# Eleven instead of ten Strassen pairs in a 256-token FFN's down projection, two by two, and re-ordered stage ends, on one Trainium2 core

## The chip, the core and the metric

One Trainium2 core runs the whole program in one launch. The metric is device microseconds (us) from launch to end, lower is better. The engines are named as in the profile: PE (TensorE matmul) with PEld (its weight loads), DVE (VectorE), ACT (ScalarE), POOL (GpSimd), and SP, whose queue issues the loads of the weights.

## The reference

One encoder layer on 256 tokens of 2048 features, all in float32. A half-step FFN, a mixer (gated linear recurrence beside windowed attention), and a second half-step FFN; RMS norms stand before and behind each.

```
x: [1, 256, 2048]     D_FF = 5632
swiglu(x, w_gate_up, w_down):
    gate, up = split(x @ w_gate_up, 2)           # 2048 -> 2 x 5632
    return (silu(gate) * up) @ w_down            # 5632 -> 2048
x = x + 0.5 * rms_norm(swiglu(rms_norm(x, g1), ...), p1)
p = rms_norm(x, gm) @ w_mix_in                   # 2048 -> 6656
x = x + rms_norm(concat(hgrn2(p), attention(p)) @ w_mix_out, pm)
x = x + 0.5 * rms_norm(swiglu(rms_norm(x, g2), ...), p2)
```

Here the change touches the product with `w_down` in both FFNs, and the stretches between stages, in which the norm of a finished stage meets the first products of the next.

## The kernel before

**Products.** An fp32 product is made of three matmuls on split operands: every weight tile `raw` is cast to a rounded part `h` by ACT (L176), DVE subtracts to get the rest `l` (L177), and PE multiplies h·h, h·l and l·h (`three`, L423 in the profile). A plain *pair* `u` is 256 rows of weights (two tiles of 128 rows) times 1024 columns: 2 tiles x 2 blocks of 128 tokens x 2 blocks of 512 columns x 3, that is 24 matmuls of 128x512. A pair can instead go as a *seven* (`seven`): a scheme of Strassen's kind on the 2x2x2 blocks takes seven block products instead of eight, so 21 matmuls. For that, DVE forms sums of weight blocks first: one addition of 1024 columns (L455) and two of 512 (L459, L461), each in place in `raw`, and each followed by a further cast and split. Its left operands are sums of the activations: they are formed once (`sums_of`, L380 to L384, three DVE operations) and split into `sp` at each use, unless the pair is in `keep`, in which case the split of run 0 is kept for run 1. Four of the seven products gather in banks of their own, which `fold` (L489 and on, eight DVE additions and an ACT copy) adds into the result behind the last seven of a run.

**Down projection.** `Pairs` walks the 22 pairs of `w_down` twice: run 0 makes columns 0 to 1023, run 1 columns 1024 to 2047. `orders` gives the order of the pairs in each run, by hand. The even pairs below 20 (`MIXED`, ten of them) are sevens; the lists alternate a plain pair and a seven, up to the last few. With `AHEAD`, a seven begins the split of the plain pair behind it, so its DVE work is mixed with that pair's. The last two pairs of run 1 are held back for the end (`HELD`). All loads are issued by SP into a ring of `raw` buffers.

**Stage ends.** `finish` writes out by hand what stands in a row on PE, DVE and ACT. It finishes the four banks of run 1 one by one, squares and sums them (`squares`), multiplies by the gain (`gains`), adds the normed result to the residual X in blocks of 128x512 (`update(m, q)`, L666), turns X by PE transposes (`turned`, L210), and takes from the turned blocks the two split parts of X^T: the upper ones on ACT (`hi`, L227), the lower ones on DVE (`lo`, L232). Between these, `lead` brings the next stage's weights (`lead.more` splits them) and its first products (`lead.pieces`, L352 to L354 in the mixer's). There are two such ends, in which a next stage follows: behind the first FFN (end 1) and behind the mixer (end 2). `pre_stats` squares X (`jk`, L249 on ACT, eight blocks) for the next norm; in the FFNs its result reaches PE by `spread`, a product with a diagonal matrix `dg` (L267, L268).

Of the kernel before, what the change touches and what calls it, by code (L numbers as in the profile page):

```python
# [37 lines left out]
def hymba_layer_kernel(  # L38
# [204 lines left out]

    def pre_stats_now():
        for m in range(2):
            ssq = stat.tile([P, 4], F32, tag="ssq", name=nm("ssq"))
            for q in range(4):
                jk = stat.tile([P, 512], BF16, tag="jk", name=nm("jk"), bufs=1)
                nc.scalar.activation(  # L249
                    jk, res["X"][:, m, q * 512 : (q + 1) * 512], AF.Square, accum_out=ssq[:, q : q + 1]  # L250
                )
            r = rsqrt_of(ssq, 1.0 / D, EPS)
            last["rs2"] = nc.vector.tensor_copy(rs2[:, m : m + 1], r)
# [286 lines left out]
    class Pairs(Blocks):  # L540
# [90 lines left out]
        def finish(self, mul, post, new_x=None, gain=None, lead=None):  # L631
# [88 lines left out]
            def lo(m, q):  # L720
                take_lo(m, q, gain, xt, banks[m, q])

            with tc.manual_schedule(engines=ordered):
                products(0, 0, every)
                squares(0, 0)
                gains(0, 0)
                products(0, 1, every)
                squares(0, 1)
                update(0, 0)
                gains(0, 1)  # L730
                products(1, 0, every)
                lead.more(0)
                update(0, 1)
                squares(1, 0)
                gains(1, 0)
                products(1, 1, slice(0, 3))

                def took(m, q):
                    hi(m, q)
                    lo(m, q)  # L740

                turned(0, 0)
                took(0, 0)
                products(1, 1, slice(3, None))
                turned(0, 1)
                squares(1, 1)
                took(0, 1)
                update(1, 0)
                update(1, 1)
                lead.more(1)  # L750
                first, second = lead.pieces(0, xt), lead.pieces(1, xt)
                next(first)
                next(first)
                turned(1, 0)
                took(1, 0)
                gains(1, 1)
                next(first)
                turned(1, 1)
                took(1, 1)
                for _ in first:  # L760
                    pass
                for m, q in ((0, 2), (1, 2), (0, 3), (1, 3)):
                    update(m, q)
                    next(second)
                    turned(m, q)
                    took(m, q)
                for _ in second:
                    pass
# [19 lines left out]
    MIXED = range(0, 20, 2)  # L788
# [48 lines left out]
    def ffn(gated, w_dn, post_gain, again, gain=None, lead=None, aside=None):  # L837

        with ExitStack() as st:
# [10 lines left out]
            def sums_room(u):  # L850
                n = MIXED.index(u)
                if n == 0:
                    where_X_was.append(xp.tile([P, 8, 4, P], F32, tag="X", name=nm("sums")))
                if n < 8:
                    return where_X_was[0][:, n]
                return work.tile([P, 4, P], F32, tag=f"su{n}", name=nm("su"))
# [57 lines left out]
            for g in range(NG):  # L914
# [18 lines left out]
                [1, 0, 3, 2, 5, 4, 7, 6, 9, 8, 11, 10, 13, 12, 15, 14, 17, 16, 18, 19, 20, 21],  # L933

                [1, 0, 3, 2, 5, 4, 7, 6, 9, 8, 11, 10, 12, 13, 14, 15, 16, 18, 17, 19, 20, 21],
            ]
            rows = Pairs(w_dn, orders, hts, sums, work, post_gain, keep=(10, 12, 16))
# [18 lines left out]
    with tc.manual_schedule():  # L956
# [54 lines left out]
        gated.parts[1] = split(raws[0])  # L1011
        turned(0, 1)
# [6 lines left out]
        gated.parts[2] = split(raws[1])  # L1019
        for k in range(2):  # L1020
# [506 lines left out]
```

## Time and profile before

| | us |
|---|---|
| median of 3 runs | 1853.87 (1853.67 to 1853.91) |
| the profiled execution | 1853.69 |
| its span, first to last instruction | 1851.4 |
| PE busy | 1836.2 |
| DVE busy | 1559.9 |
| ACT busy | 1079.3 |
| DMA moved | 365.78 MB, a mean of 198 GB/s |

The profiled execution is 0.18 us below the median, and 2.29 us of it lie outside the span. The stages can be told by the weights that are loaded and by the lines: FFN 1's gate and up projection to about 488 us, its down projection in two runs to about 599 and 704, end 1 to 745, the mixer to 1123 with end 2 behind it to 1155, FFN 2's gate and up to 1614, its down projection to the end. PE is busy nearly throughout, so the time is read as PE's work plus the gaps in it. A gap is read from the starts: matmuls that follow one another start 0.227 us apart, and what a start is later than that is lost. A bracket behind a row names the idle time ahead of it and what ended it.

### The profile page before, as it was taken

Reading aid. Unit: us, or ns where it says so; the run is one execution under the profiler, and the core shown is the slowest. Engines: PE = TensorE matmul, PEld = TensorE weight load, DVE = VectorE, ACT = ScalarE, POOL = GpSimd, SP = SyncE. Lnnn points to the kernel's source line nnn. Section 1 sums busy time; section 2 is a strip of 40 time slices with the busy share of each in tenths; the row PEclk is TensorE's granted clock in tenths of the full one; section 3 lists DMA queues with packets and bytes.
Section 4 is the critical chain, followed back from the end, with each engine's and each line's share of the span. In section 5 each row is a group of like instructions: output and inputs, shape, how many; then the busy total and the mean of one; then the engine's idle time right before and its main releaser. Section 6 shows DMA issues by size and latency. Waiting matters only on the chain.

```text
span 1851.4 us, 23247 instructions
## 1 busy us (share of the span) xinstructions
PE 1836.2 (99%) x8670; PEld 1533.2 (83%) x8670; DVE 1559.9 (84%) x1956; ACT 1079.3 (58%) x1429; POOL 20.6 (1%) x39
## 2 busy tenths in 40 slices
PE   9999999999999999999999999999999999999998
PEld 7888888888888887888888887888888888888886
DVE  7988888888899998577787788888888788899997
ACT  6555555555565655577677655655555555566563
POOL 1000000000000000000000000000000000000000
PEclk9999999999999999999999999999999999999999
DMA  7555555555565565555565555565555555555564
GB/s 253 205 197 189 205 204 182 182 190 200 190 227 212 198 255 197 194 177 166 169 186 157 172 208 200 182 214 186 210 206 194 204 184 206 190 183 207 217 249 156
DMA packets 180881, 365.78 MB, mean 198 GB/s; under 512 B 9257, under 2 KB 56449, under 8 KB 180001
## 3 DMA queue, kind: packets, MB, share of 16 engines
q1 hardware_dynamic: 180416, 364.17, 56.5%
q8 instruction: 68, 1.11, 0.2%
q14 instruction: 45, 0.36, 0.1%
q0 software_dynamic: 352, 0.14, 0.0%
HBM read 360.06 MB, written 4.21 MB: 197 GB/s over the span
## 4 chain that ended last, share of the span: by engine, by line
PE 95%; DVE 2%; ACT 1%; DMA 1%; issue 1%; POOL 0%; SPq 0%; DVEq 0%; ACTq 0%; POOLq 0%
PE pa L423 40%; PE pb L423 37%; PE pa L299 8%; PE pa L304 4%; PE pa L354 1%; PE pa L352 1%; PE pa L353 1%; DVE l L177 1%; PE pa L896 0%; PE pb L896 0%; ACT xt L227 0%; PE pb L1270 0%; PE pb L1248 0%; PE pb L1396 0%; ACT jk L249 0%
## 5 line engine op out<-in xcount | busy, mean ns | idle before, releaser
L176 ACT CAST h<-raw 128x1024 fp32r<-128x1024 f32 (+1 forms) x789 | 796.3, 1029 | 626.9 <-PE pb L423 344.4
L177 DVE TENSOR_TENSOR l<-raw,h 128x1024 fp32r<-128x1024 f32 (+1 forms) x789 | 923.3, 1193 | 202.7 <-ACT h L176 169.2
L423 PE MATMUL pa<-h,xt 128*128 128x512 f32 x1248 | 431.5, 392 | 0.0
L423 PE MATMUL pb<-h,xt 128*128 128x512 f32 x1168 | 407.2, 390 | 0.0
L423 PEld LDWEIGHTS pa<-h,xt 128*128 128x128 f32 x1248 | 234.4, 188 | 48.8 <-ACT h L176 0.8
L423 PEld LDWEIGHTS pb<-h,xt 128*128 128x128 f32 x1168 | 219.2, 188 | 45.5
L423 PE MATMUL pa<-l,xt 128*128 128x512 f32 x624 | 243.2, 390 | 0.0
L423 PE MATMUL pb<-l,xt 128*128 128x512 f32 x584 | 227.3, 389 | 0.0
L299 PE MATMUL pa<-xt,h 128*128 128x512 f32 x672 | 164.7, 394 | 0.0
L423 PE MATMUL pa<-h,ht 128*128 128x512 f32 x464 | 162.7, 389 | 0.0
L423 PE MATMUL pb<-h,ht 128*128 128x512 f32 x464 | 162.6, 389 | 0.0
L299 PEld LDWEIGHTS pa<-xt,h 128*128 128x128 f32 x672 | 123.0, 188 | 23.6
L423 PEld LDWEIGHTS pa<-l,xt 128*128 128x128 f32 x624 | 117.4, 188 | 23.8 <-DVE l L177 0.5
L423 PEld LDWEIGHTS pb<-l,xt 128*128 128x128 f32 x584 | 109.7, 188 | 22.6
L455 DVE TENSOR_TENSOR raw<-raw 128x1024 f32<-128x1024 f32 x84 | 102.8, 1223 | 2.2
L423 PEld LDWEIGHTS pa<-h,ht 128*128 128x128 f32 x464 | 87.1, 188 | 18.2
L423 PEld LDWEIGHTS pb<-h,ht 128*128 128x128 f32 x464 | 87.1, 188 | 18.0
L304 PE MATMUL pa<-xt,l 128*128 128x256 f32 x672 | 91.5, 285 | 0.0
L423 PE MATMUL pa<-l,ht 128*128 128x512 f32 x232 | 90.3, 389 | 0.0
L423 PE MATMUL pb<-l,ht 128*128 128x512 f32 x232 | 90.3, 389 | 0.0
L304 PEld LDWEIGHTS pa<-xt,l 128*128 128x128 f32 x672 | 87.1, 191 | 3.2
L423 PE MATMUL pb<-h,sp 128*128 128x512 f32 x176 | 61.8, 390 | 0.0
(280 smaller groups left out, 2133.0 us busy)
## 6 DMA issues: line engine op xcount, KB each, us to landing
raw<-in_w_ffn_gate_up_dram SPq DMA_DIRECT2D x350, 512.0 KB, 4.7
raw<-in_w_ffn_down_dram SPq DMA_DIRECT2D x88, 1024.0 KB, 5.0
raw<-in_w_mix_in_dram SPq DMA_DIRECT2D x52, 1024.0 KB, 4.9
raw<-in_w_mix_out_dram SPq DMA_DIRECT2D x16, 1024.0 KB, 5.0
pg<-in_post_norm_ffn_dram SPq DMA_DIRECT2D x4, 512.0 KB, 5.8
X<-in_x_dram SPq DMA_DIRECT2D x2, 1024.0 KB, 7.3
bias<-row SPq DMA_DIRECT2D x16, 128.0 KB, 4.6
kept<-X SPq DMA_DIRECT2D x2, 1024.0 KB, 4.8
```

The lines of the kernel that those rows point to most:

```text
L176: nc.scalar.copy(hi, src)
L177: nc.vector.tensor_tensor(lo, src, hi.bitcast(F32), ALU.subtract)
L299: nc.tensor.matmul(slot[f], weights(hs, kk, f), xcol(xt, k), start=(k == 0), stop=(k == KT - 1))
L304: nc.tensor.matmul(slot[f][:, 0:T], weights(ls, kk, f), xcol(xt, kh * 8 + kk, 0), start=False, stop=False,)
L352: nc.tensor.matmul(dst, xh, h[:, o : o + n], start=(k == 0), stop=False)
L353: nc.tensor.matmul(dst, xh, l[:, o : o + n], start=False, stop=False)
L354: nc.tensor.matmul(dst, xl, h[:, o : o + n], start=False, stop=(k == KT - 1))
L423: nc.tensor.matmul(self.bank(at), lhs, rhs, start=(n == 1), stop=n in (ends, self.of[at]), skip_group_check=n > ends,)
L455: nc.vector.tensor_tensor(four[:, 0:2], four[:, 0::3], four[:, 1:2].to_broadcast([P, 2, 512]), ALU.add)
```

## The change

**Down projection.** `MIXED` has eleven pairs, so pair 20 becomes a seven as well, in both runs of both FFNs. The orders no longer alternate: in run 0 the sevens 2 and 4, 8 and 10, 14 and 16, 18 and 20 stand two in a row, in run 1 2 and 4, 8 and 10, 14 and 16, 18 and 20. `keep` has two pairs instead of three. The sums of pair 20 have a place of their own (`su` in the far pool), reserved by `sums[NU - 2] = None` before `Pairs` asks which pairs are sevens.

**Ends.** The four lower parts of a block can be taken two by two (`js`), and the updates of X are placed between them, ahead of the first products of the next stage that need them; `lead.more` comes earlier.

**Squares.** `square_x(m, q)` squares one block of X at any place; `pre_stats_now` squares only the blocks that are left. Four of eight are squared within the ends, two of eight near the start of the kernel.

```
-    MIXED = range(0, 20, 2)
+    MIXED = range(0, 22, 2)
...
+                if u >= NU - 2:
+                    return far["pool"].tile([P, 4, P], F32, tag="su", name=nm("su"), bufs=1)
...
-                [1, 0, 3, 2, 5, 4, 7, 6, 9, 8, 11, 10, 12, 13, 14, 15, 16, 18, 17, 19, 20, 21],
+                [1, 0, 3, 2, 4, 5, 6, 7, 8, 10, 9, 12, 11, 14, 16, 13, 18, 20, 15, 17, 19, 21],
             ]
-            rows = Pairs(w_dn, orders, hts, sums, work, post_gain, keep=(10, 12, 16))
+
+            sums[NU - 2] = None
+            rows = Pairs(w_dn, orders, hts, sums, work, post_gain, keep=(4, 10))
...
+    squared = {}
+    def square_x(m, q):
+        if m not in squared:
+            squared[m] = (stat.tile([P, 4], F32, tag="ssq", name=nm("ssq")), set())
+        ssq, done = squared[m]
+        if q not in done:
+            done.add(q)
...
     def pre_stats_now():
         for m in range(2):
...
-            r = rsqrt_of(ssq, 1.0 / D, EPS)
+                square_x(m, q)
+            r = rsqrt_of(squared.pop(m)[0], 1.0 / D, EPS)
...
                 products(1, 1, slice(0, 3))
...
+                hi(0, 1)
+                square_x(0, 0)
+                square_x(0, 1)
+                lo(0, 0, (2, 3))
+                lo(0, 1, (0, 1))
+                update(1, 0)
+                lo(0, 1, (2, 3))
+                update(1, 1)
+                update(0, 2)
+                update(0, 3)
...
+                gains(1, 1)
+                lo(1, 1)
+                update(1, 2)
+                update(1, 3)
+                for m, q in ((0, 2), (1, 2), (0, 3), (1, 3)):
+                    next(second)
+                    turned(m, q)
                     hi(m, q)
                     lo(m, q)
...
                 for m, q in ((0, 2), (1, 2), (0, 3), (1, 3)):
-                    update(m, q)
-                    next(second)
-                    turned(m, q)
-                    took(m, q)
...
         gated.parts[1] = split(raws[0])
+        square_x(0, 0)
...
         gated.parts[2] = split(raws[1])
+        square_x(1, 0)
```

**DVE, the last sevens of run 1 in FFN 1, before.** `la` and `l` are rests of weight tiles, `raw<-raw` the additions on weight blocks, here of pairs 16 (`raw_5603`) and 18 (`raw_5645`); the last three rows belong to plain pairs.

```order
L461 TENSOR_TENSOR raw_5603<-raw_5603 128x512
L177 TENSOR_TENSOR la_5648<-raw_5645,ha_5647 128x512
L455 TENSOR_TENSOR raw_5645<-raw_5645 128x1024
L177 TENSOR_TENSOR l_5621<-raw_5603,h_5620 128x1024
L177 TENSOR_TENSOR l_5653<-raw_5645,h_5652 128x1024
L459 TENSOR_TENSOR raw_5645<-raw_5645 128x512
L177 TENSOR_TENSOR l_5658<-raw_5645,h_5657 128x1024
L461 TENSOR_TENSOR raw_5645<-raw_5645 128x512
L177 TENSOR_TENSOR l_5663<-raw_5645,h_5662 128x1024
L177 TENSOR_TENSOR l_5697<-raw_5694,h_5696 128x1024
L177 TENSOR_TENSOR l_5701<-raw_5694,h_5700 128x1024
L177 TENSOR_TENSOR l_5731<-raw_5728,h_5730 128x1024
```

The same place after, with pairs 18 (`raw_5631`) and 20 (`raw_5676`):

```order
L471 TENSOR_TENSOR raw_5631<-raw_5631 128x512
L177 TENSOR_TENSOR la_5679<-raw_5676,ha_5678 128x512
L465 TENSOR_TENSOR raw_5676<-raw_5676 128x1024
L177 TENSOR_TENSOR l_5649<-raw_5631,h_5648 128x1024
L177 TENSOR_TENSOR l_5684<-raw_5676,h_5683 128x1024
L177 TENSOR_TENSOR l_5689<-raw_5676,h_5688 128x1024
L469 TENSOR_TENSOR raw_5676<-raw_5676 128x512
L471 TENSOR_TENSOR raw_5676<-raw_5676 128x512
L177 TENSOR_TENSOR l_5694<-raw_5676,h_5693 128x1024
L177 TENSOR_TENSOR l_5728<-raw_5725,h_5727 128x1024
```

In both, the last split of the last seven (`l_5663`, `l_5694`) stands right behind its last addition, with an ACT cast of the sum between the two. What moved: both middle splits now stand ahead of the two 512-wide additions, where one of them stood between them, and after `l_5694` only plain pairs' splits and `fold` are left.

**DVE, end 1, before.** `X` rows are the updates, `xt` rows the lower parts of X^T, `l` rows the splits of the mixer's weights.

```order
L666 SCALAR_TENSOR_TENSOR X_5795<-y_5738,r_5850,X_5795 128x512
L177 TENSOR_TENSOR l_6126<-raw_6123,h_6125 128x1024
L177 TENSOR_TENSOR l_6130<-raw_6123,h_6129 128x1024
L232 SCALAR_TENSOR_TENSOR xt_5814<-pa_5984,cols,xt_5814 128x128 x4
L666 SCALAR_TENSOR_TENSOR X_5795<-y_5738,r_5910,X_5795 128x512
L177 TENSOR_TENSOR l_6160<-raw_6157,h_6159 128x1024
L232 SCALAR_TENSOR_TENSOR xt_5814<-pb_6004,cols,xt_5814 128x128 x4
L666 SCALAR_TENSOR_TENSOR X_5795<-y_5738,r_5850,X_5795 128x512
L177 TENSOR_TENSOR l_6164<-raw_6157,h_6163 128x1024
```

The same stretch after:

```order
L232 SCALAR_TENSOR_TENSOR xt_5844<-pa_5932,cols,xt_5844 128x128 x2
L676 SCALAR_TENSOR_TENSOR X_5826<-y_4904,r_5943,X_5826 128x512
L232 SCALAR_TENSOR_TENSOR xt_5844<-pa_5932,cols,xt_5844 128x128 x2
L676 SCALAR_TENSOR_TENSOR X_5826<-y_4904,r_5943,X_5826 128x512
L676 SCALAR_TENSOR_TENSOR X_5826<-y_5769,r_5885,X_5826 128x512 x2
L232 SCALAR_TENSOR_TENSOR xt_5844<-pb_5982,cols,xt_5844 128x128 x4
L629 TENSOR_TENSOR y_5769<-pb_4989,pg_5824 128x512
L232 SCALAR_TENSOR_TENSOR xt_5844<-pb_6001,cols,xt_5844 128x128 x4
L676 SCALAR_TENSOR_TENSOR X_5826<-y_5769,r_5943,X_5826 128x512 x2
L177 TENSOR_TENSOR l_6161<-raw_6154,h_6160 128x1024
```

The last four updates have moved from between the weight splits and the second half's lower parts to ahead of them.

**ACT, near the start of the kernel, before and after.** `h` rows are casts of weights, `xt` rows the upper parts of X^T.

```order
L176 CAST h_211<-raw_137 128x1024
L227 ACTIVATE xt_123<-pa_215,gain_102 128x128 x4
L227 ACTIVATE xt_123<-pb_220,gain_102 128x128 x4
L176 CAST h_265<-raw_142 128x1024
L176 CAST h_269<-raw_142 128x1024
L176 CAST h_396<-raw_393 128x1024
```

```order
L176 CAST h_211<-raw_137 128x1024
L254 ACTIVATE jk_216,ssq_215<-X_75 128x512
L227 ACTIVATE xt_123<-pa_218,gain_102 128x128 x4
L227 ACTIVATE xt_123<-pb_223,gain_102 128x128 x4
L176 CAST h_268<-raw_142 128x1024
L176 CAST h_272<-raw_142 128x1024
L254 ACTIVATE jk_277,ssq_276<-X_75 128x512
L176 CAST h_396<-raw_393 128x1024
```

Two squares (`jk`) of eight have moved ahead of casts and upper parts; the other six stand some rows later, where all eight stood.

## Rows read from the trace of the kernel before

**Rows 1.** Windows: span and busy us per engine, run 0 and run 1.

```profile
core 0: us, PE busy (x) PEld busy (x) DVE busy (x) ACT busy (x) POOL busy (x), PEclk, DMA share, GB/s
494.60:594.10 99.50, 99.50 (x441) 82.10 (x440) 96.61 (x107) 60.76 (x68) 0.00 (x0) 1.00 0.58 212
594.20:704.10 109.90, 109.90 (x486) 91.01 (x485) 104.16 (x112) 67.32 (x79) 0.00 (x0) 1.00 0.63 226
```

**Rows 2.** Chain that ended last: start, us, engine, line, a pair's 24 matmuls.

```profile
1831.94 5.44 PE pa L423 x24
```

**Rows 3.** Groups by form, run 1, DVE: count, busy us, mean ns, idle before.

```profile
L177 DVE TENSOR_TENSOR l<-raw,h 128x1024 fp32r<-128x1024 f32 x55 | 66.1, 1219 | 4.3 <-ACT h L176 4.1
L455 DVE TENSOR_TENSOR raw<-raw 128x1024 f32<-128x1024 f32 x10 | 12.2, 1224 | 0.3
L177 DVE TENSOR_TENSOR sp<-sums,sp 128x512 fp32r<-128x512 f32 x5 | 3.4, 684 | 0.0
```

**Rows 4.** Timeline of DVE late in run 1: start, us, operation, [idle <-releaser].

```profile
689.39 4.63 DVE L177 TENSOR_TENSOR l<-raw,h 128x1024 fp32r<-128x1024 f32 x4 [1.20 <-ACT h L176]
698.07 0.69 DVE L500 TENSOR_TENSOR pa<-pa,y 128x512 f32<-128x512 f32 x1
698.67 0.69 DVE L501 TENSOR_TENSOR pb<-pb,y 128x512 f32<-128x512 f32 x1
```

**Rows 5.** One line's instructions, L380: duration min/median/max in ns.

```profile
L380 DVE TENSOR_TENSOR su<-z x4: 416/418/419, 410.8 to 1580.2; 128x256 f32<-128x256 f32 x4
```

**Rows 6.** Timeline: a last split in run 0, its reader; that of run 1.

```profile
574.61 1.23 DVE L177 TENSOR_TENSOR l<-raw,h 128x1024 fp32r<-128x1024 f32 x1
...
580.17 0.39 PE L423 MATMUL pb<-l,sp 128*128 128x512 f32 x1
...
692.37 0.39 PE L423 MATMUL pb<-l,sp 128*128 128x512 f32 x1
```

**Rows 7.** Timeline of PE around the two spreads, FFN 1 and FFN 2.

```profile
39.24 0.39 PE L423 MATMUL pa<-h,xt 128*128 128x512 f32 x1
40.32 0.71 PE L268 MATMUL pb<-dg,ones 128*128 128x128 f32 x4 [0.69 <-DVE dg L267]
...
1167.37 0.39 PE L423 MATMUL pb<-h,xt 128*128 128x512 f32 x1
1168.52 0.71 PE L268 MATMUL pb<-dg,ones 128*128 128x128 f32 x4 [0.76 <-DVE dg L267]
```

**Rows 8.** One line's instructions, the squares of X on ACT, duration in ns.

```profile
L249 ACT ACTIVATE jk<-X x24: 620/632/649, 29.6 to 1166.0; 128x512 bf16<-128x512 f32 x24
```

**Rows 9.** Timeline of ACT near the start of the kernel.

```profile
14.88 1.14 ACT L227 ACTIVATE xt<-pa,gain 128x128 fp32r<-128x128 f32 x4 [0.93 <-PE pa L210]
```

**Rows 10.** Timeline of PE in end 1, two transposes of X.

```profile
718.98 0.39 PE L354 MATMUL pa<-h,xt 128*128 128x512 f32 x1
719.85 0.66 PE L210 MATMUL pb<-ident,X 128*128 128x128 f32 x4 [0.49 <-DVE X L666]
...
731.92 0.39 PE L354 MATMUL pa<-h,xt 128*128 128x512 f32 x1
733.52 0.66 PE L210 MATMUL pa<-ident,X 128*128 128x128 f32 x4 [1.21 <-DVE X L666]
```

**Rows 11.** Timeline of PE in end 2, a transpose of X.

```profile
1137.41 0.39 PE L423 MATMUL pa<-h,xt 128*128 128x512 f32 x1
1138.28 0.66 PE L210 MATMUL pb<-ident,X 128*128 128x128 f32 x4 [0.49 <-DVE X L666]
```

**Rows 12.** Timeline of ACT and PE early in FFN 2's run 0.

```profile
1632.49 2.00 ACT L176 CAST h<-raw 128x1024 fp32r<-128x1024 f32 x2 [4.62 <-DMA raw<-in_w_ffn_down_dram]
...
1634.69 0.61 PE L423 MATMUL pb<-h,sp 128*128 128x512 f32 x2
1635.99 0.50 PE L423 MATMUL pb<-l,sp 128*128 128x512 f32 x1 [0.68 <-DVE l L177]
```

**Rows 13.** Windows: the stretch behind end 1's longest wait, columns as in Rows 1.

```profile
733.50:745.00 11.50, 11.48 (x55) 9.55 (x56) 8.62 (x17) 9.54 (x23) 2.19 (x5) 1.00 0.67 228
```

More of the change, by code (lines that the diff above doesn't have):

```diff
@@ L242, in pre_stats @@
             pre_stats_now()
+    squared = {}
[5 more added lines that the diff above has]
+            done.add(q)
+            jk = stat.tile([P, 512], BF16, tag="jk", name=nm("jk"), bufs=1)
+            nc.scalar.activation(
+                jk, res["X"][:, m, q * 512 : (q + 1) * 512], AF.Square, accum_out=ssq[:, q : q + 1]
+            )
     def pre_stats_now():
         for m in range(2):
-            ssq = stat.tile([P, 4], F32, tag="ssq", name=nm("ssq"))
             for q in range(4):
[L248 to L251, printed above, removed]
-            r = rsqrt_of(ssq, 1.0 / D, EPS)
+                square_x(m, q)
+            r = rsqrt_of(squared.pop(m)[0], 1.0 / D, EPS)
             last["rs2"] = nc.vector.tensor_copy(rs2[:, m : m + 1], r)
@@ L718, in hi, with lo @@
                 take_hi(m, q, gain, xt, banks[m, q])
-            def lo(m, q):
-                take_lo(m, q, gain, xt, banks[m, q])
+            def lo(m, q, js=range(4)):
+                take_lo(m, q, gain, xt, banks[m, q], js)
             with tc.manual_schedule(engines=ordered):
@@ L726, in finish @@
                 gains(0, 0)
+                lead.more(0)
                 products(0, 1, every)
                 squares(0, 1)
+                lead.more(1)
                 update(0, 0)
@@ L731, in finish @@
                 products(1, 0, every)
-                lead.more(0)
                 update(0, 1)
@@ L736, in finish @@
                 products(1, 1, slice(0, 3))
-                def took(m, q):
+                turned(0, 0)
+                hi(0, 0)
+                products(1, 1, slice(3, None))
+                lo(0, 0, (0, 1))
+                turned(0, 1)
+                squares(1, 1)
+                hi(0, 1)
[8 more added lines that the diff above has]
+                update(0, 3)
+                first, second = lead.pieces(0, xt), lead.pieces(1, xt)
+                for _ in range(3):
+                    next(first)
+                turned(1, 0)
+                hi(1, 0)
+                next(first)
+                lo(1, 0)
+                turned(1, 1)
+                hi(1, 1)
+                square_x(1, 0)
+                square_x(1, 1)
+                gains(1, 1)
[5 more added lines that the diff above has]
+                    turned(m, q)
                     hi(m, q)
                     lo(m, q)
[L742 to L762, printed above, removed]
-                    update(m, q)
-                    next(second)
-                    turned(m, q)
-                    took(m, q)
-                for _ in second:
+                for _ in (*first, *second):
                     pass
@@ L932, in ffn @@
             orders = [
-                [1, 0, 3, 2, 5, 4, 7, 6, 9, 8, 11, 10, 13, 12, 15, 14, 17, 16, 18, 19, 20, 21],
-                [1, 0, 3, 2, 5, 4, 7, 6, 9, 8, 11, 10, 12, 13, 14, 15, 16, 18, 17, 19, 20, 21],
-            ]
-            rows = Pairs(w_dn, orders, hts, sums, work, post_gain, keep=(10, 12, 16))
+                [1, 3, 0, 5, 2, 4, 7, 6, 9, 8, 10, 11, 12, 13, 14, 16, 15, 18, 20, 17, 19, 21],
+                [1, 0, 3, 2, 4, 5, 6, 7, 8, 10, 9, 12, 11, 14, 16, 13, 18, 20, 15, 17, 19, 21],
+            ]
+            sums[NU - 2] = None
+            rows = Pairs(w_dn, orders, hts, sums, work, post_gain, keep=(4, 10))
             rows.half_gain(far["pool"])
@@ L1019, in hymba_layer_kernel @@
         gated.parts[2] = split(raws[1])
+        square_x(1, 0)
         for k in range(2):
```

## The prediction

> **What bounds the kernel now.** I first read the windows over the two runs of FFN 1's down projection [rows 1]: PE is busy 99.50 of 99.50 us and 109.90 of 109.90, so the time there is PE's number of matmuls times their pace. The pace comes from the chain that ended last: 24 matmuls of a plain pair in 5.44 us, or 0.227 each [rows 2]. The reader should then look at VectorE in the same windows: 96.61 and 104.16 us. It is the second engine, 2.89 and 5.74 us from being the first. So whatever takes matmuls from PE and gives additions to VectorE is limited by these two differences, and by how early VectorE finishes an operand before PE reads it, its lead. Outside the runs PE has a few gaps: one at each spread of the norm [rows 7], and some at the two ends, where a transpose waits for an update of X [rows 10, 11]. These are what the other two parts of the change can take.
>
> **Part 1: twelve matmuls fewer.** Pair 20 goes as 21 matmuls instead of 24, in two runs of two FFNs: 4 x 3 = 12, at 0.227 that is -2.72 us. All of it lies on PE, which is the path. The loads are the same in size and number; only their order on SP's queue changes.
>
> **Part 1, what VectorE pays.** Operations of 1024 columns follow one another at (4.63 - 1.22) / 3 = 1.137 us, those of 512 at 0.60 [rows 3, 4]. A plain pair needs two splits, 2.27 us. A seven needs the addition L455 and three splits of 1024, and four operations of 512 (`la`, L459, L461, `sp`): 4 x 1.137 + 4 x 0.60 = 6.95 us. The new seven costs VectorE 4.68 us more in each run. Run 0 also gets the activation sums of pair 20, since these are formed when the down projection has begun: three operations of at most 0.42 [rows 5], between 0.6 and 1.25, I take 1.0. In run 1 one pair fewer has its split kept: +0.60. PE meanwhile is 3 x 0.227 = 0.68 shorter. So VectorE falls behind PE by 4.68 + 1.0 + 0.68 = 6.36 us more in run 0, and by 4.68 + 0.60 + 0.68 = 5.96 in run 1.
>
> What is there to meet this? First the lead. In run 0 a seven's last split ends at 574.61 + 1.23 = 575.84 and is read at 580.17: 4.33 us early. In run 1 that of the last seven ends at about 690.61 (the first of the four in a row) and is read at 692.37: 1.76 early [rows 4, 6]. Second the idle time, 2.89 and 5.74. If none of the idle time can be used, 6.36 - 4.33 = 2.03 and 5.96 - 1.76 = 4.20 are left, 6.2 us for one FFN. If all of it can, nothing is left: 2.03 is below 2.89 and 4.20 below 5.74. A gain is excluded here, as PE has no gap in these windows that could close. I take the middle, 3.1 for one FFN: of run 1's idle time 4.1 us stands ahead of splits that wait for ACT's cast [rows 3]. Where VectorE is late these casts are done by the time it comes and the idle time vanishes by itself; but the last wait of 1.20 [rows 4] is bound to a chain (last addition, cast, split) that the new order keeps, and two sevens in a row leave no plain pair between them in which VectorE could catch up. For two FFNs that is +6.2, with 0 and 12.4 as ends.
>
> One load is late already: in FFN 2's run 0 ACT sits 4.62 us until a weight tile lands, and PE loses 1635.99 - 1634.69 - 2 x 0.227 = 0.85 us [rows 12]. I count that as it is, neither gone nor doubled. With less lead another late load would pass through to PE; 0 to 1 us for one FFN goes into the range.
>
> **Part 2: the ends.** A gap is the distance of two starts less 0.227. In end 1 the transposes lose 719.85 - 718.98 - 0.227 = 0.64 and 733.52 - 731.92 - 0.227 = 1.37 [rows 10]; in end 2 one loses 0.64 [rows 11]. VectorE had put the updates behind splits of weights and lower parts of X^T; now the updates come first. Sum 2.65. What is late next is a lower part: the products of the next stage read them, and VectorE now does two or four updates ahead of some. The nearest price is that of an update behind a transpose, 0.64; I leave half of it, 0.3, in all, so -2.35. The ends of this term: -2.65, and 0 if the lower parts lose what the updates gain. Moving the weight splits earlier (`lead.more`) costs nothing as long as VectorE has nothing late there; that is covered by PE's products of the two held pairs, 5.44 us each, and costs one split of 1.14 where it isn't.
>
> **Part 3: the squares.** The two spreads lose 40.32 - 39.24 - 0.227 = 0.85 and 1168.52 - 1167.37 - 0.227 = 0.92 [rows 7]. They end a chain that begins with the last square of X on ACT. A square takes 0.63 [rows 8]; two of eight are taken out of the chain's head at the start, 1.26, four of eight at end 2, 2.5. Both exceed the gap, so both gaps go: -1.77. What is late next is the matmul ahead of the spread, which is PE's own. Where they go to: ACT had 0.93 us of idle time ahead of the first upper parts at the start [rows 9], which hides the first square; the second, and those in the ends, stand where ACT is at 9.54 of 11.50 us [rows 13], which leaves room for three of 0.63. If the cover is missing, each costs at most its 0.63. I take 0.
>
> **The sum.** Against the profiled execution of 1853.69 us, which is 0.18 below the median: -2.72 - 2.35 - 1.77 = -6.84, and +6.2 for VectorE, together -0.6: 1853.05, and on the median's footing 1853.2. The parts nearly cancel. About 0.2% (3.7 us) is what a measurement of this kernel can tell from no change; this is well inside.
>
> **Rivals.**
>
> *VectorE holds.* Sevens are doubled where the lead was large, 4.33 us, and most idle time is used, so one FFN loses 0.8 us or less instead of 3.1. Then 1853.87 - 6.84 + 1.6 = 1848.6, at best 1847.0. From a loss of (6.84 - 3.7) / 2 = 1.6 us for one FFN downward it counts as faster. For it: the windows have more idle time than is needed. Against it: a lead of 1.76 late in run 1, and 1.2 of wait that order can't remove.
>
> *VectorE is the bound in both runs.* The idle time is bound to ACT's casts and PE's releases, none can be used, and the loss is 6.2 for one FFN: 1853.87 - 6.84 + 12.4 = 1859.4, with a late load on top 1861. It decides for slower from (6.84 + 3.7) / 2 = 5.3 us for one FFN. The place is run 1 from pair 14 on, where two doubles follow with one pair between. For it: after three sevens of 6.95 us against PE's 4.77 VectorE has lost 6.5, more than any lead seen. Against it: the plain pairs after that give back 3.2 each (5.44 less 2.27).
>
> *The ends don't gain.* The lower parts are late where the updates were: 1853.2 + 2.35 = 1855.6, still within 0.2%.
>
> *The clock.* In the stretch behind the longest gap of 1.37 us the granted clock is 1.00, the upper of the two levels (2.4 GHz) [rows 13]. If new waits of VectorE in run 1 let it fall to the lower (1.2 GHz), every plain pair passed at it costs 5.44 us more, so one pair in each FFN gives 1853.2 + 10.9 = 1864. The Trainium skill, TensorE: Matmul & The Clock Gate, section "HAM oscillation — how this bites in real kernels", says that a TensorE that sits idle for long between groups of matmuls falls back to the lower clock each time, and pays again on the way up; by that rule the doubled sevens would be dearer than their waits. By the trace, whose gaps of up to 1.37 us left the clock at 1.00, it would not bite here, as I expect no new wait above 1.5.
>
> **How the numbers follow.** The forecast, a loss of 1.6 to 5.3 for one FFN with the ends gained, 0.42; the same without the gain at the ends, 0.11; VectorE holds 0.27; VectorE is the bound 0.18; the clock 0.02. So faster by over 0.2% 0.27, within 0.2% 0.53, slower 0.20. The range runs from 1848.0, where VectorE loses 0.5 for one FFN, to 1859.0, a loss of 6.0: it leaves out some 0.1 on each side.
>
> **What would show it.** In the profile after, the windows over the runs should show VectorE at nearly their whole length and PE for the first time below it; PE's waits there should name the split (L177) as their releaser, largest in run 1 behind pairs 16 and 20, about 1 us at one place and 3 us in one FFN. In the two spreads PE should start within 0.3 us of the matmul ahead; in end 1 no transpose should wait above 0.4. I would be wrong if PE waits nowhere in the runs (VectorE holds), if the waits in one FFN exceed 5.3 us (VectorE is the bound), if the granted clock is below 1.00 behind a wait, or if the gaps at the ends have moved to the products that read lower parts.

## The result, and the profile after

The changed kernel takes 1857.06 us (median of 20 runs, 1856.13 to 1858.20) against 1854.16 for the kernel before (20 runs): a ratio of 1.0015, interval 1.0008 to 1.0022. It is slower by 2.9 us. The forecast was 1853.2, a gain of 0.6. The profiled execution takes 1856.80 with a span of 1854.5, 3.1 more than before.

To see where the time went I summed PE's gaps by stage in both traces: the distance of two starts less the usual one for that shape, counted where it exceeds 0.1 us.

| stage | before, us | after, us |
|---|---|---|
| start of the kernel (0 to 36) | 2.05 | 1.45 |
| first spread | 0.95 | 0 |
| down projection of FFN 1 | 0.11 | 6.20 |
| end 1 | 3.05 | 0.43 |
| mixer | 2.69 | 3.38 |
| end 2 and second spread | 2.25 | 0.42 |
| gate and up of FFN 2 | 0.25 | 0 |
| down projection of FFN 2 | 1.07 | 5.66 |
| sum | 12.4 | 17.5 |

Gaps grow by 5.1 us, and twelve matmuls fewer give 2.7 back: +2.4 of the 3.1; the rest is in steps below 0.1. So the ends and spreads gained 5.4, more than was forecast, and the down projections lost 10.7, twice as much.

The windows of the two runs of FFN 1 after the change, columns as in [rows 1]:

```profile
489.00:592.50 103.50, 103.10 (x455) 83.83 (x453) 101.28 (x115) 64.66 (x77) 0.00 (x0) 1.00 0.53 196
592.50:706.00 113.50, 111.04 (x478) 88.83 (x479) 108.54 (x120) 67.81 (x83) 0.00 (x0) 1.00 0.61 226
```

PE is no longer busy throughout. But the reader should see VectorE, the third busy time: in run 1 it is busy 108.54 of 113.50, so it sits idle for 5.0 us in a stretch in which PE waits for it. Before it was idle for 5.7 [rows 1]. The total hardly fell when VectorE fell behind; what it is made of changed.

Where it sits is shown by the waits of that window (engine, line, what was waited for: us in total, times, longest):

```profile
ACT h L176 <- DVE raw L465: 16.0, 7, 3.0
ACT h L176 <- DVE raw L471: 15.9, 8, 3.2
...
DVE l L177 <- ACT h L176: 4.3, 5, 1.4
...
PEld pb L433 <- ACT h L176: 2.1, 3, 1.6
PEld pb L433 <- DVE l L177: 2.0, 5, 0.7
```

ACT waits for VectorE's own additions (L465, L471), and VectorE waits 4.3 us for ACT. To tell what these waits are, one has to go a step further back, to what ACT's cast had waited for. Timelines of ACT and VectorE in run 1, first before the change, then after:

```profile
650.92 1.05 ACT L176 CAST h<-raw 128x1024 fp32r<-128x1024 f32 x1 [0.98 <-PE pa L423]
652.00 1.23 DVE L177 TENSOR_TENSOR l<-raw,h 128x1024 fp32r<-128x1024 f32 x1 [0.59 <-ACT h L176]
```

```profile
650.58 2.00 ACT L176 CAST h<-raw 128x1024 fp32r<-128x1024 f32 x2 [2.15 <-DVE raw L471]
651.66 2.36 DVE L177 TENSOR_TENSOR l<-raw,h 128x1024 fp32r<-128x1024 f32 x2 [0.57 <-ACT h L176]
...
659.77 2.96 ACT L176 CAST h<-raw 128x1024 fp32r<-128x1024 f32 x3 [1.71 <-DMA raw<-in_w_ffn_down_dram]
660.86 2.36 DVE L177 TENSOR_TENSOR l<-raw,h 128x1024 fp32r<-128x1024 f32 x2 [1.37 <-ACT h L176]
```

Before, five waits of 0.53 to 0.59 us in run 1, 2.9 together, were for casts that had waited for PE, as at 650.92; after the change 0.15 of this kind is left. In its place come four waits for casts that had waited for VectorE's own last addition (L471), three of 0.57 and one of 1.17, again 2.9 together; before there was one of 1.20 [rows 4]. They stand at the ends of the four doubles. Run 0 has three more of 0.57. The longest wait, 1.37, is of a third kind: the cast had waited for a load of weights. In FFN 2 the same load costs VectorE 0.89, and PE nothing.

The largest single gap of PE, at the last double (18 and 20), shows the chain in one place: timelines of VectorE, ACT and PE.

```profile
692.43 0.69 DVE L469 TENSOR_TENSOR raw<-raw 128x512 f32<-128x512 f32 x1
693.15 0.69 DVE L471 TENSOR_TENSOR raw<-raw 128x512 f32<-128x512 f32 x1
695.01 3.50 DVE L177 TENSOR_TENSOR l<-raw,h 128x1024 fp32r<-128x1024 f32 x3 [1.17 <-ACT h L176]
...
693.93 4.85 ACT L176 CAST h<-raw 128x1024 fp32r<-128x1024 f32 x5 [3.15 <-DVE raw L471]
...
693.45 0.39 PE L433 MATMUL pb<-h,sp 128*128 128x512 f32 x1
695.03 0.50 PE L433 MATMUL pb<-h,sp 128*128 128x512 f32 x1 [1.19 <-ACT h L176]
```

The addition ends at 693.84, ACT's cast begins at 693.93 and takes 1.05, VectorE's split and PE's matmul begin at 695.0. PE started its last matmul at 693.45: 695.03 - 693.45 - 0.227 = 1.35 us are lost there, and VectorE did nothing for 1.17 of them. PE here waits for the cast itself, not for the split. Of the 6.2 us of FFN 1, PE lost 3.0 behind casts on ACT, 1.3 behind splits for which VectorE had waited 0.57, 1.0 behind `fold`, 0.6 behind the late load, and the rest in steps of about 0.1.

The ends and spreads answer to [rows 7], [rows 10] and [rows 11]. Timeline of PE after: both spreads, end 1's first products, and two of its transposes.

```profile
38.13 0.39 PE L433 MATMUL pb<-h,xt 128*128 128x512 f32 x1
38.36 0.60 PE L278 MATMUL pb<-dg,ones 128*128 128x128 f32 x4
...
1166.52 0.39 PE L433 MATMUL pb<-h,xt 128*128 128x512 f32 x1
1166.74 0.60 PE L278 MATMUL pb<-dg,ones 128*128 128x128 f32 x4
...
720.30 0.40 PE L363 MATMUL pa<-l,xt 128*128 128x512 f32 x1
720.84 0.50 PE L364 MATMUL pa<-h,xt 128*128 128x512 f32 x1
...
728.26 0.60 PE L210 MATMUL pa<-ident,X 128*128 128x128 f32 x4
731.97 0.60 PE L210 MATMUL pa<-ident,X 128*128 128x128 f32 x4
```

The spreads follow without a gap, the transposes have no wait in brackets, and in end 1 one gap is left, 720.84 - 720.30 - 0.227 = 0.31, ahead of a product that reads a lower part of X^T (L364). End 2 has one of the same size at 1137.0.

### The profile page after: what moved, and what is told of

It is laid out like the page before. It is cut to its first block, busy times and chain, and to the rows that moved or that the text cites. A ratio compares the mean times of both kernels' runs of the same rounds, so it can differ in the third digit from the quotient of the medians.

```text
span 1854.5 us, 23272 instructions
## 1 busy us (share of the span) xinstructions
PE 1838.1 (99%) x8658; PEld 1528.3 (82%) x8658; DVE 1576.5 (85%) x1988; ACT 1085.4 (59%) x1445; POOL 21.4 (1%) x39
## 4 chain that ended last, share of the span: by engine, by line
PE 75%; DVE 18%; issue 3%; ACT 2%; DMA 2%; DVEq 0%; SPq 0%; POOL 0%; ACTq 0%; POOLq 0%
PE pa L433 29%; PE pb L433 27%; DVE l L177 9%; PE pa L309 8%; PE pa L314 4%; DVE raw L465 3%; ACT h L176 1%; DVE raw L469 1%; DVE raw L471 1%; DVE la L177 1%; DMA raw<-in_w_ffn_down_dram 1%; PE pa L364 1%; PE pa L363 1%; PE pa L362 1%; DVE sp L177 1%
## 5 line engine op out<-in xcount | busy, mean ns | idle before, releaser
L433 PE MATMUL pa<-h,ht 128*128 128x512 f32 x440 | 156.6, 391 | 0.4 <-ACT h L176 0.4
L433 PE MATMUL pb<-h,ht 128*128 128x512 f32 x440 | 155.8, 391 | 0.9 <-DVE pb L511 0.7
L465 DVE TENSOR_TENSOR raw<-raw 128x1024 f32<-128x1024 f32 x88 | 107.6, 1222 | 1.8
L433 PEld LDWEIGHTS pa<-h,ht 128*128 128x128 f32 x440 | 82.3, 188 | 20.1 <-ACT h L176 2.9
L433 PEld LDWEIGHTS pb<-h,ht 128*128 128x128 f32 x440 | 82.6, 188 | 19.2 <-DVE pb L511 2.4
L433 PE MATMUL pb<-l,ht 128*128 128x512 f32 x220 | 85.7, 390 | 0.0
L433 PE MATMUL pa<-l,ht 128*128 128x512 f32 x220 | 85.7, 390 | 0.0
L433 PE MATMUL pb<-h,sp 128*128 128x512 f32 x192 | 69.1, 394 | 2.4 <-ACT h L176 2.4
```

The lines of the kernel that those rows point to most:

```text
L433: nc.tensor.matmul(self.bank(at), lhs, rhs, start=(n == 1), stop=n in (ends, self.of[at]), skip_group_check=n > ends,)
L465: nc.vector.tensor_tensor(four[:, 0:2], four[:, 0::3], four[:, 1:2].to_broadcast([P, 2, 512]), ALU.add)
```

## Experiments

"Gaps" are PE's in the two down projections, summed as above, FFN 1 and FFN 2, each from one profiled execution. Two such executions of one kernel (changed, ten sevens) differ by 1.06 us in FFN 2, so differences of about 1 us are not read here.

| kernel | us | ratio to before (95%) | gaps, us |
|---|---|---|---|
| changed | 1857.06 | 1.0015 (1.0008 to 1.0022) | 6.20, 5.66 |
| ends and squares only | 1847.99 | 0.9963 (0.9951 to 0.9976) | 0.11, 1.09 |
| down projection only | 1862.78 | 1.0046 (1.0031 to 1.0061) | 5.59, 5.87 |
| changed, ten sevens | 1846.59, again 1847.40 | 0.9960 (0.9945 to 0.9974), again 0.9961 | 0, 1.06, again 0, 0 |
| changed, one addition left out | 1843.86 | 0.9943 (0.9928 to 0.9957) | 0, 0 |
| last double parted | 1860.67 | 1.0033 (1.0022 to 1.0045) | 6.03, 8.43 |
| both orders others | 1861.95 | 1.0041 (1.0026 to 1.0056) | 6.99, 8.94 |
| ten sevens, no early squares | 1847.43 | 0.9966 (0.9952 to 0.9979) | 0, 0.28 |
| ten sevens, squares at the start only | 1846.40 | 0.9958 (0.9943 to 0.9973) | 0, 1.35 |
| GpSimd takes a split | 1885.08 | 1.0167 (1.0152 to 1.0182) | 21.9, 18.9 |
| additions put aside | 1845.07 | 0.9949 (0.9934 to 0.9964) | 1.68, 0 |
| early addition, eleven sevens | 1846.33 | 0.9956 (0.9941 to 0.9971) | 1.12, 1.42 |
| early addition, ten sevens | 1845.68 | 0.9952 (0.9936 to 0.9969) | 0, 0 |

### The two parts apart

```
-    MIXED = range(0, 22, 2)
+    MIXED = range(0, 20, 2)
...
-            sums[NU - 2] = None
-            rows = Pairs(w_dn, orders, hts, sums, work, post_gain, keep=(4, 10))
+            rows = Pairs(w_dn, orders, hts, sums, work, post_gain, keep=(10, 12, 16))
```

with both `orders` of the kernel before:

> The changed kernel with the down projection put back as before: ten sevens, alternating orders, the three kept pairs; the re-ordered ends and the early squares stay. Summed over the gaps of PE in the two traces, the ends, spreads and the start lose about 6 us less after the change. If the parts are independent (my theory), this kernel is at 1854.2 - 6 = 1848 us, and its ends show gaps of 0.3 at most. Rival: the ends gain only because the down projection before them ends late and the weights of the next stage have been loaded meanwhile; then the gaps return, and the time is 1851 to 1854.

1847.99 us, 6.6 less than before on the same chip, as the theory had it; the rival is out. Left in the down projections is the late load of before, 0.88. The other part alone, the kernel before with the edits of `MIXED`, `orders`, `keep` and the room for pair 20:

> The kernel before with the down projection alone changed (eleven sevens, doubled orders, two kept pairs). PE's new gaps in the two down projections sum to about 11.6 us after the change, against 2.7 saved by twelve matmuls fewer. Theory (parts independent): 1854.2 + 11.6 - 2.7 = 1863 us, 1862 if the late load of before is gone as it is after. Rival (the ends share in the loss): 1858 to 1860.

1862.78, as expected. The same gap as in the changed kernel stands at the last double:

```profile
694.97 0.39 PE L423 MATMUL pb<-h,sp 128*128 128x512 f32 x1
696.54 0.50 PE L423 MATMUL pb<-h,sp 128*128 128x512 f32 x1 [1.19 <-ACT h L176]
```

Ends and squares are worth -6.6 here, the down projection +8.2; the sum, +1.6, is 1.3 off the changed kernel's +2.9, more than the 0.8 between two medians of one kernel (ten sevens), but within the intervals. PE's gaps in the down projections, 11.5 here and 11.9 in the changed kernel, agree. So the parts are independent as far as can be told; an interaction of 1 us is not excluded.

### Quantity or order

```
-    MIXED = range(0, 22, 2)
+    MIXED = range(0, 20, 2)
...
-            sums[NU - 2] = None
```

on the changed kernel, its orders kept:

> The changed kernel with ten sevens instead of eleven, in the changed kernel's doubled orders (pair 20 goes plain at its place). Theory (the amount of VectorE's work costs, not the doubling): VectorE has 4.7 us less in each run and its lead holds, so PE's gaps in the runs fall below 1 us for one FFN and the time is 1848 to 1850 us. Rival (the doubling costs, since two sevens in a row leave no plain pair to catch up in): gaps stay above 3 us for one FFN and the time is 1855 to 1860.

1846.59, against the rival's 1855 to 1860, and somewhat below the theory's 1848 to 1850. With ten sevens, doubled as after, run 0 and run 1 of FFN 1 have no gap:

```profile
488.60:595.00 106.40, 106.40 (x476) 88.17 (x475) 104.05 (x116) 66.31 (x77) 0.00 (x0) 1.00 0.58 207
595.00:704.50 109.50, 109.50 (x485) 90.67 (x484) 104.47 (x112) 66.07 (x78) 0.00 (x0) 1.00 0.67 241
```

In FFN 2 the sum was 1.06 in this execution and 0 in a later one. So doubling by itself costs little or nothing; pair 20's seven does, be it by its amount of work or by its place in the last double. Next, less work for VectorE at eleven sevens:

```
-            nc.vector.tensor_tensor(
-                four[:, 0:2], four[:, 0::3], four[:, 1:2].to_broadcast([P, 2, 512]), ALU.add
-            )
+            if not self.AHEAD:
+                nc.vector.tensor_tensor(
+                    four[:, 0:2], four[:, 0::3], four[:, 1:2].to_broadcast([P, 2, 512]), ALU.add
+                )
```

> The changed kernel with VectorE's 1024-wide addition left out of every seven of the down projection (the lower half of the weights is split as loaded, so this part of the computation is missing): VectorE has 11 x 1.14 = 12.5 us less in each run, PE and ACT the same work. Theory (VectorE's amount of work): all of PE's gaps in the runs but those of the last seven's chain go, so 11.6 falls to about 3 and the time is 1848 to 1849 us. Rival (the chain of last addition, cast and split behind doubled sevens, whatever VectorE's load): the gaps with ACT's cast as releaser, 2.4 us for one FFN, and those of the splits stay and the time is 1852 to 1857.

1843.86, below what either theory said: no gap is left, the last seven's chain included. With 12.5 us less to do in a run VectorE could be so far ahead that the chain ends before PE comes; that was not shown, and the edit also takes a link out of the chain, since the cast behind this addition no longer waits for it. At this point I took the amount of VectorE's work for the whole cause. Two kernels with other orders, run 1 with its last double parted,

```
-                [1, 0, 3, 2, 4, 5, 6, 7, 8, 10, 9, 12, 11, 14, 16, 13, 18, 20, 15, 17, 19, 21],
+                [1, 0, 2, 3, 4, 6, 5, 8, 7, 10, 12, 9, 14, 11, 16, 18, 13, 20, 15, 17, 19, 21],
```

> The changed kernel with another order in run 1 only: the sevens 0 and 2, 4 and 6, 10 and 12, 16 and 18 are doubled, and pair 20 stands alone behind a plain pair; in the changed kernel the last double, 18 and 20, ends in gaps of about 2.3 us (1.35 and 0.38 twice, with restarts) whose releaser is ACT's cast. Theory (VectorE owes its time whatever the order): the gaps move to earlier sevens and the sum for one run stays at 4 to 5 us, the time at 1856 to 1858. Rival (the wait is made by the last double itself): 2.3 us in each FFN go, 1852 to 1853.

and the same with run 0 nearly alternating,

```
-                [1, 3, 0, 5, 2, 4, 7, 6, 9, 8, 10, 11, 12, 13, 14, 16, 15, 18, 20, 17, 19, 21],
+                [1, 0, 3, 2, 5, 4, 7, 6, 9, 8, 11, 10, 13, 12, 14, 15, 16, 18, 17, 20, 19, 21],
```

> The changed kernel with eleven sevens, run 0 alternating as long as it can (only 12 and 14, 16 and 18 are near each other) and run 1 as in the kernel with the parted last double. Theory (amount of work): 1855 to 1860 us. Rival (the doubled orders of run 0 are the fault): 1852 or less, as run 0's gaps of about 2 us in each FFN go as well.

came out at 1860.67 and 1861.95, 3.6 and 4.9 slower than the changed kernel. The gap at the last double went, as told, and others came: the parted order loses 6.03 and 8.43. Both rivals are out, and so are the theory's bounds, 1856 to 1858 and 1855 to 1860: with equal work the order moved the sum by up to 4 us. So the amount was not all.

### The chain

The same work for VectorE, but no cast that waits for its two 512-wide additions:

```
+            to22 = to21 = None
+            if self.AHEAD:
+                to22 = to21 = stat.tile([P, 512], BF16, tag="jk", name=nm("jk"), bufs=1)
-            nc.vector.tensor_tensor(b22, b11, b22, ALU.add)
+            nc.vector.tensor_tensor(b22 if to22 is None else to22, b11, b22, ALU.add)
             upper = split_half(raw, 0)
-            nc.vector.tensor_tensor(b21, b22, b21, ALU.add)
+            nc.vector.tensor_tensor(b21 if to21 is None else to21, b22, b21, ALU.add)
```

> The changed kernel, eleven sevens, with the same number of additions on VectorE, but the two 512-wide ones of every seven of the down projection write into a spare tile instead of the weights, so no cast has to wait for them (the last third of each seven is made of unsummed weights, so this part of the computation is wrong). It asks why VectorE sat idle for 5 us in run 1 while PE waited 6. Theory (the idle time is a chain on VectorE's own additions: addition, ACT's cast, split, and so cannot be filled when VectorE is late): VectorE's idle time and PE's gaps shrink together, gaps of 1 to 3 us for one FFN instead of 6, 1847 to 1852 us. Rival (only the amount of VectorE's work counts): the gaps stay, 1855 to 1858.

1845.07, 12 us below the changed kernel, below the theory's own bounds. VectorE's timeline at the place of the last double:

```profile
686.05 0.69 DVE L472 TENSOR_TENSOR jk<-raw 128x512 bf16<-128x512 f32 x1
686.78 0.69 DVE L474 TENSOR_TENSOR jk<-raw 128x512 bf16<-128x512 f32 x1
687.39 6.90 DVE L177 TENSOR_TENSOR l<-raw,h 128x1024 fp32r<-128x1024 f32 x6
```

The additions take the same 0.69, and six splits follow without a break. This suggests a kernel that computes everything: the last addition ahead of the split that follows the second sum, so that ACT casts while VectorE splits.

```
-            upper = split_half(raw, 0)
-            nc.vector.tensor_tensor(b21, b22, b21, ALU.add)
+            part = raw[:, 0:1024]
+            upper = tuple(
+                p.tile([P, 1024], F32R, tag=t, name=nm(t)) for p, t in ((hip, "h"), (lop, "l"))
+            )
+            nc.scalar.copy(upper[0], part)
+            summed21 = nc.vector.tensor_tensor(b21, b22, b21, ALU.add)
+            with tc.issue_after(summed21.ins):
+                nc.vector.tensor_tensor(upper[1], part, upper[0].bitcast(F32), ALU.subtract)
```

> The changed kernel, eleven sevens, same orders, same work on every engine: in every seven VectorE now makes the last 512-wide addition ahead of the split that follows the second sum, so ACT casts the last sum while VectorE does that split. Theory (the idle time of VectorE behind its own additions is what turns the eleventh seven into a loss): PE's gaps in the runs fall from 6 to 1 to 2 us for one FFN, the time to 1843 to 1848 us. Rival (the amount of VectorE's work): 1855 to 1858, since no work is taken away.

1846.33: 10.7 us off the changed kernel with not one operation fewer. Its windows over the two runs of FFN 1:

```profile
488.00:591.50 103.50, 103.13 (x459) 85.16 (x458) 102.87 (x118) 66.98 (x80) 0.00 (x0) 1.00 0.56 205
591.50:703.00 111.50, 111.50 (x491) 91.59 (x490) 110.36 (x122) 69.62 (x84) 0.00 (x0) 1.00 0.62 228
```

and VectorE's timeline at the place of the last double:

```profile
687.31 0.69 DVE L475 TENSOR_TENSOR raw<-raw 128x512 f32<-128x512 f32 x1
687.92 1.22 DVE L477 TENSOR_TENSOR l<-raw,h 128x1024 fp32r<-128x1024 f32 x1
689.20 5.77 DVE L177 TENSOR_TENSOR l<-raw,h 128x1024 fp32r<-128x1024 f32 x5
```

VectorE's idle time in run 1 fell from 4.96 to 1.14 us and PE is busy 111.50 of 111.50. Where the changed kernel has addition, 1.17 idle, split, there is now addition, split, split. This shows the cause: with the same orders and the same work, the place of the last addition takes away 9.3 of the 11.9 us of gaps. It does not part VectorE's waits from PE's own waits for the same casts; both come from that addition. The largest of the gaps that are left, 0.53 in FFN 1 and 0.78 in FFN 2, stand behind splits that VectorE reached late with no idle time right before them. With ten sevens:

> The same with ten sevens. Its runs had gaps below 1 us for one FFN already. Theory: no change against the ten-seven kernel, 1846 to 1847; if the eleven-seven kernel with the early addition is faster than this, the eleventh seven pays once the chain is hidden, by up to 2.7 us. Rival (the early addition delays the split it is put ahead of, by 0.6 each): new gaps, 1848 or more.

(the last diff on the ten-seven kernel) 1845.68, gaps of 0 and 0, faster than both kernels of the comparison (0.9952, interval 0.9936 to 0.9969). Against eleven, 1846.33, the difference is not to be told from none, and nor is it against the ten-seven kernel's 1846.59 and 1847.40. In the profiled executions the 2.7 us that the eleventh seven saves are about what its gaps, 1.12 + 1.42, take. It does not pay yet, but it is no longer a loss that can be measured.

### The squares

On the changed kernel with ten sevens, all six calls outside `pre_stats_now` taken out:

```
-                square_x(0, 0)
-                square_x(0, 1)
...
-                square_x(1, 0)
-                square_x(1, 1)
...
-        square_x(0, 0)
...
-        square_x(1, 0)
```

> The changed kernel with ten sevens (1846.6 us measured) without the six early squares: all eight are taken where the kernel before takes them; the re-ordered ends stay. Theory: the two spreads lose 0.85 and 0.92 again and 0.1 each for the restart, so 1848.6 us. Rival (the squares only move the wait elsewhere): no change, 1846.6.

1847.43, where the ten-seven kernel took 1846.59 and, measured again, 1847.40: a loss of 2 us is not there, and one of less than 0.8 can't be told. Timeline of PE at the two spreads of this kernel without early squares:

```profile
39.23 0.39 PE L433 MATMUL pa<-h,xt 128*128 128x512 f32 x1
40.94 0.38 PE L278 MATMUL pb<-dg,ones 128*128 128x128 f32 x1 [1.32 <-DVE dg L277]
...
1162.57 0.39 PE L433 MATMUL pb<-h,xt 128*128 128x512 f32 x1
1162.80 0.60 PE L278 MATMUL pb<-dg,ones 128*128 128x128 f32 x4
```

The first spread's gap is back, 1.48; the second has none. It was closed by the re-ordered end, not by squares. Taking out only the first four of these lines, those in `finish`, says the same; the ten-seven kernel ran once more beside it:

> The changed kernel with ten sevens, without the four squares within the ends; the two at the kernel's start stay. In the kernel without any early squares the first spread had its gap (1.48 us) and the second had none, so the re-ordered end alone closed the second. Theory: the four do nothing, the time is that of the ten-seven kernel, 1846.6. Rival: they are worth the 0.92 us of the second gap, 1847.5 or more.

> The changed kernel with ten sevens, once more, beside the kernel without the squares of the ends on the same chip: 1846.6 us as measured, and a gap of 0.3 at most at either spread.

1846.40 and 1847.40: the four do nothing. The last expectation failed in a detail, the first spread lost 0.60 in that execution (0 in the earlier one of this kernel, 0.42 without the four). So the two squares at the start shorten the first gap and do not always close it: with them it was between 0 and 0.60, without them 0.85 to 1.59. In the execution with 0.60 ACT had waited 0.88 us for a load of gate and up weights and began the last six squares at 30.47, in the changed kernel's, without that wait, at 29.47. But the earlier ten-seven execution has such a wait too, 0.97, and no gap, so the cause stays open.

### GpSimd as a helper

```
-            split_act(w[:, :, 0, :], w[:, :, 1, :], self.sums[u])
+            nc.scalar.copy(w[:, :, 0, :], self.sums[u])
+            nc.gpsimd.tensor_tensor(
+                w[:, :, 1, :], self.sums[u], w[:, :, 0, :].bitcast(F32), ALU.subtract
+            )
```

> The changed kernel (eleven sevens) with the low part of the split activation sums taken by GpSimd instead of VectorE, 11 operations of 128x512 in run 0 and 9 in run 1 of each FFN. One GpSimd operation of this shape on float32 takes 1.27 us in the profile of the changed kernel, VectorE's 0.60. Theory (VectorE's amount of work is what costs, and GpSimd is free): VectorE has 6.6 and 5.4 us less in the runs, about what the eleventh seven added, PE's gaps fall from 6 to 1 us in each FFN and the time is 1844 to 1847. Rival (the two engines hinder each other at the memory): VectorE waits 1.27 for each 0.60 it is spared, 20 x 0.67 = 13 us more for one FFN, and the time is 1865 to 1880.

1885.08, beyond the rival's end. Groups by form over FFN 1's down projection, GpSimd and VectorE's splits and additions:

```profile
L586 POOL TENSOR_TENSOR sp<-sums,sp 128x512 fp32r<-128x512 f32 x14 | 26.2, 1880 | 561.9 <-ACT sp L585 561.9
...
L177 DVE TENSOR_TENSOR l<-raw,h 128x1024 fp32r<-128x1024 f32 x107 | 135.0, 1285 | 9.8 <-ACT h L176 9.0
L465 DVE TENSOR_TENSOR raw<-raw 128x1024 f32<-128x1024 f32 x22 | 30.0, 1364 | 0.3
L469 DVE TENSOR_TENSOR raw<-raw 128x512 f32<-128x512 f32 x22 | 21.4, 971 | 0.5
L471 DVE TENSOR_TENSOR raw<-raw 128x512 f32<-128x512 f32 x22 | 17.2, 780 | 0.3
```

and a place where the two met, timelines of GpSimd and VectorE:

```profile
505.86 1.84 POOL L586 TENSOR_TENSOR sp<-sums,sp 128x512 fp32r<-128x512 f32 x1 [8.61 <-ACT sp L585]
...
506.58 1.66 DVE L469 TENSOR_TENSOR raw<-raw 128x512 f32<-128x512 f32 x1
```

GpSimd's operation took 1.88 on the mean of these 14, where the one of that shape in the changed kernel (L683) took 1.27, and VectorE's 128x512 addition 0.97 on the mean instead of 0.69. VectorE was spared some 20 x 0.60 = 12 us in each FFN. It lost about 18.5: 22 additions by 0.28, 22 by 0.09, 22 of 1024 by 0.14 and 107 splits by 0.07. These 6.5 us net are less than half of what PE's gaps grew by in FFN 1, 21.9 against 6.2. A further 5.2 are 26 matmuls at the lower clock, which started 0.427 us apart instead of 0.227 (below); the rest was not taken apart.

## Why the prediction was wrong, point by point

**What bounds it.** Right: PE by its number of matmuls, VectorE as the second engine, and the change lives on the difference. **Twelve matmuls fewer**, -2.72: right, as the matmul counts and the balance above show.

**What VectorE pays.** This is the step that failed: +6.2 for both FFNs was the middle between no loss and 12.4, and the measured gaps are 6.20 and 5.66, 11.9 together, near the upper end. The middle rested on the sentence that "where VectorE is late these casts are done by the time it comes and the idle time vanishes by itself". It was true of the casts that wait for PE: 2.9 us of such idle time in run 1 fell to 0.15. It is false of a cast of a sum: that starts when VectorE's own addition ends, so it is late when VectorE is late. The prediction counted one such wait, of 1.20 [rows 4]; after the change there are four in run 1 and three in run 0, and PE itself waits for some of these casts. So in run 1 most of the old idle time was used, and 1.7 us more of waits for casts of sums and 1.37 behind a late load came in its place (4.96 against 5.74 in all). That the gaps are so near to the 6.2 reckoned for "none can be used" is in part luck, as that reckoning kept the old idle time. With the last addition moved ahead VectorE's idle time fell to 1.14, and the gaps to 1.1 and 1.4. The prediction also put nothing on `fold`, which cost 1.0 in FFN 1.

**The late load** of [rows 12], 0.85: the prediction counted it as staying. It stands in the kernel before and in the one with the ends alone, and is gone in both kernels with the new orders and eleven sevens, so it went with the orders. That helped by about 1 us and makes the miss on VectorE's term a little larger. Another load came late in run 1 instead, at 0.56 in FFN 1 and nothing in FFN 2, within the 0 to 1 that the range had for it.

**The ends**, -2.35: right and somewhat too small. End 1 went from 3.05 to 0.43 and end 2 from 1.22 to 0.42; the prediction had left out the gaps below 0.5. What is late next is a lower part, as said, 0.31 at each end.

**The squares**, -1.77: right in the sum, since both gaps went, wrong in the reason for the second, which the ends closed. The squares within the ends are worth nothing that could be measured.

**Rivals.** "VectorE is the bound in both runs" comes nearest: the waits passed the 5.3 us for one FFN that were its sign, and its place was named (run 1 from pair 14 on; the largest gap is behind 20). Of the other signs, VectorE at nearly its whole length did not come (108.54 of 113.50), and the largest wait of PE names ACT's cast instead of the split. Its reason holds only in part, since the idle time bound to PE's releases was used. Its price was 1859.4, and the time was 1857.06, since the ends gave more and the late load went. It had a chance of 0.18. The time lies within the range and within the 0.2% held likeliest, but it rose where a small gain was forecast; that it stayed in the range is partly luck, since the ends' larger gain and the lost late load made up for part of the miss on VectorE. **The clock** stayed at 1.00 in both runs' windows, so that rival is out for this kernel. But its reason, no new wait above 1.5, is not safe: in the kernel with GpSimd the clock fell behind waits of 0.77 and 1.22 (last section).

## What to carry to other kernels

Before counting an engine's idle time as room for new work, look at what ended each wait, and at what that step had itself waited for. Idle time that goes back to another engine's release was room here, and was used. Idle time that goes back to the engine's own output, sent to another engine and returned (addition, cast, split), is latency, and it comes anew wherever nothing else stands between. Such a loop is hidden by putting the step that goes out ahead of a step that needn't wait, which here was worth 10.7 us with no work removed. And a change of several parts is measured by its parts: here one was worth -6.6 and the other +8.2.

## What the runs showed of the hardware

VectorE and GpSimd hinder each other when both read two float32 operands from SBUF: the 128x512 operation of GpSimd took 1.27 us in the changed kernel and 1.88 on the mean beside VectorE's splits and additions, and VectorE's addition, of 0.69 in the changed kernel, took 1.66 where the two met. The Trainium skill, SBUF — State Buffer, section "SBUF: two separate sides", says that a VectorE operation with two SBUF inputs and a GpSimd operation that reads SBUF lock each other out for a whole instruction. The trace agrees in that VectorE lost more than it was spared.

The clock, which was 1.00 over all four runs of the changed kernel's down projections, did fall in the kernel with GpSimd. Timeline of PE in that kernel:

```profile
589.82 0.39 PE L433 MATMUL pb<-h,sp 128*128 128x512 f32 x1
592.21 0.49 PE L433 MATMUL pb<-h,sp 128*128 128x512 f32 x1 [2.01 <-ACT h L176]
593.47 0.79 PE L433 MATMUL pb<-l,sp 128*128 128x512 f32 x1 [0.76 <-DVE l L177]
```

The windows there, columns as in [rows 1]:

```profile
590.00:593.50 3.50, 0.73 (x3) 0.22 (x2) 2.33 (x4) 2.39 (x3) 0.00 (x0) 0.88 0.00 0
593.50:597.00 3.50, 3.50 (x8) 2.77 (x9) 3.50 (x4) 2.50 (x4) 0.92 (x1) 0.50 0.64 211
```

PE was busy 0.73 of 3.50 us in two waits, and the granted clock behind them is 0.50, the lower of the two levels (1.2 GHz): its matmuls then started 0.427 us apart instead of 0.227. This is the rival on the clock, met here behind waits of 2.16 and 1.03 us in a row. In the same execution the clock fell at two more places of FFN 1, behind waits of 0.77 and 1.22 (at 678) and of 1.12 and 1.03 (at 712), and in FFN 2 behind 2.17 and 1.03 (at 1736). The single gap of 1.35 in the changed kernel did not bring it about, nor did one of 1.59 ahead of the first spread in the kernel with the down projection alone. In the mixer, which the change doesn't touch, the gap ahead of one transpose was between 0.22 and 1.04 us from one kernel's profile to another's (the kernel with GpSimd left out, which changes the mixer too).
